# Down-projection of a decoder layer: inputs and weights get buffers of their own, splits are issued ahead, and the preparation of weight sums is spread over 16 steps per half

## The chip, the cores and the metric

One Trainium2 chip, one of its cores. The number is the device time of one execution of the whole program in microseconds (us); before, the median of 3 runs was 3280.65 us (3274.83 to 3296.78).

The engines as the profile names them: PE does the matmuls (PEld loads the 128x128 operand of one), DVE and POOL do elementwise work, ACT copies and applies functions, SP issues the DMAs. Each executes its own instructions in program order and waits on semaphores of the others.

## The reference

A decoder layer on x of 2048 x 1024 in float32: four token mixers, an output projection, a layer norm, and then the feed-forward part, which is what the change touches:

```python
ALPHA = (2.0 * DEPTH) ** 0.25
x = _layer_norm(ALPHA * x + mix, ln1_w[l], ln1_b[l])
h = jnp.square(jax.nn.relu(x @ w_up[l]))            # w_up: 1024 x 4096
x = _layer_norm(ALPHA * x + h @ w_down[l], ln2_w[l], ln2_b[l])   # w_down: 4096 x 1024
```

## The kernel before

**Stages.** The mixers, the output projection and the first norm take the span up to about 1815 us. The up-projection follows in two halves of the tokens (`ffn_up(0)` and `ffn_up(1)`, 16 steps each), then the down-projection (`ffn_down`, 32 steps), which begins with its first matmul at 2518.87 us and whose last matmul ends near 3279.4 us.

**Strassen-Winograd.** Both projections use one level of it: 7 block products P1 to P7 instead of 8. The combinations of h that the products need are written to DRAM by the up-projection as `H7[half][product]` (the profile calls these arrays H0P and H1P). Four of the seven weight operands are sums of blocks of w_down: `ffn_t(f)` loads four raw tiles for one row block f, adds on DVE and POOL, and stores four tiles into `TD` (TDP in the profile). It is called 16 times between steps of the up-projection, 4 times in the first half (s = 12 to 15) and 12 times in the second (s = 1 to 12).

**Float32 by two parts.** A 128x512 float32 tile is split: a copy on ACT makes the high part (`hh`, `z`, `x0h`, `x1h`; line 135), and a subtraction on DVE, every third time on POOL, makes the low part (`hl`, `z`, `x0l`, `x1l`; line 115). A product is then 4 blocks of the contraction x 3 matmuls (hi·hi, hi·lo, lo·hi) = 12 matmuls of 128x512 into one PSUM bank.

**A step of `ffn_down`.** Step i has half i//16, v = i%16//4 (which quarter of the contraction) and p = i%4 (which pair of token tiles). It runs the products in the order P1, P6, P2, P7, P5, P4, P3; product number m = 7i + 0..6. Each product needs one input tile of H7 (raw tile by DMA, then split) and four weight tiles (8 with their low parts), which stay for 4 steps; the products change their weights at different steps (`OFF`). The weights' split tiles are not double-buffered: 16 pairs x1 for P1, P6, P4, P3 and 12 pairs x0 for P2, P7, P5. Over 32 steps there are 7 + 16 + 16 + 16 = 55 changes of 4 tiles. P1's result is copied to SBUF on ACT (`wh<-bank`), the others go through 7 DVE operations that read a bank, and 4 adds on POOL, into the y tiles. At v = 0 the y tiles are loaded with x; at v = 3 `lnorm2` normalises and stores both token tiles (ACT squares, 8 DVE operations, a power on POOL).

**What sets the order.** Tiles come from pools by name and rotate through a fixed number of places; an instruction that writes a place waits until the place's earlier readers are done. In `ffn_down` all raw tiles, inputs and weights alike, rotate through 7 places (3 named `xr`, 4 named `wl`; line 1389 issues the DMA). `prod` issues the load and the split of its own input directly ahead of its matmuls; behind the matmuls of the last product that uses a set of weights it issues loads and splits of the next set. Input splits go by turns to two `z2` tiles and to 6 pairs `hh`/`hl`. A scheduler may move instructions when the program is built.

Of the kernel before, what the change touches and what calls it, by code (L numbers as in the profile page):

```python
# [18 lines left out]
P = 128  # L19
# [65 lines left out]
class Body:  # L85
# [1205 lines left out]
        W["P3"] = put(a12)  # L1291
        return W

    def ffn_up(self, hf, X, between):

        fw = self.fw
        XN = {"P1": "B11", "P2": "B21", "P3": "B22", "P4": "T4", "P5": "T1", "P6": "T2", "P7": "T3"}

        def prod(W, n):
            ps = self.slot("pu", [P, 512])  # L1300
            wh, wl = W[n]
            for k in range(4):
                xh, xl = X[XN[n]][k]
                ks = slice(k * P, k * P + P)
                for i, (a, b) in enumerate(((wh, xh), (wh, xl), (wl, xh))):
                    self.mm(ps, a[:, ks], b, start=(k == 0 and i == 0), stop=(k == 3 and i == 2))
            return ps

        def relu2(r):
            self.act(r, r, AF.Relu)  # L1310
            self.act(r, r, AF.Square)

        for s in range(16):
            def out(n, r):
                self.nc.sync.dma_start(self.H7[hf][n][s // 4][:, :, s % 4, :], r.rearrange("p (q t) -> p q t", q=4))

            W = self.ffn_w(s)
            c11, u2, u3, c22 = (self.t(fw, n, [P, 512], bufs=i) for n, i in (("q1", 2), ("u2", 2), ("u3", 1), ("c", 1)))
            self.copy("a", c11, prod(W, "P1"))
            self.add("v", u2, c11, prod(W, "P6"))  # L1320
            self.add("v", c11, c11, prod(W, "P2"))
            relu2(c11)
            out("P1", c11)
            p5 = prod(W, "P5")
            self.add("v", u3, u2, prod(W, "P7"))
            self.add("v", u2, u2, p5)
            self.add("v", c22, u3, p5)
            relu2(c22)
            out("P4", c22)
            self.add("v", u3, u3, prod(W, "P4"))  # L1330
            relu2(u3)
            out("P2", u3)
            self.add("v", u2, u2, prod(W, "P3"))
            relu2(u2)

            self.add("v", c22, u2, c22)
            out("P5", c22)
            self.sub("g", u2, c11, u2)
            out("P7", u2)
            self.sub("v", c11, c22, c11)  # L1340
            out("P6", c11)
            self.sub("g", u3, u3, c11)
            out("P3", u3)
            between(s)

    def ffn_t(self, f):

        nc, w = self.nc, self.ap["w_down"]
        b12, t1, b22 = self.raw(w[f][:, 512:]), self.raw(w[f][:, :512]), self.raw(w[f + 16][:, 512:])
        b21 = self.t(self.of, "x1t", [P, 2, 512], bufs=1)[:, 0]  # L1350
        nc.sync.dma_start(b21, w[f + 16][:, :512])
        self.sub("v", t1, b12, t1)
        nc.sync.dma_start(self.TD["P5"][f], t1)
        self.sub("g", b12, b22, b12)
        nc.sync.dma_start(self.TD["P7"][f], b12)
        self.sub("v", b22, b22, t1)
        nc.sync.dma_start(self.TD["P6"][f], b22)
        self.sub("g", b21, b21, b22)
        nc.sync.dma_start(self.TD["P4"][f], b21)

# [3 lines left out]
    def ffn_down(self):  # L1366
# [5 lines left out]
        with ExitStack() as es:  # L1372
            fs = es.enter_context(tc.tile_pool(name="fs", bufs=1, side="right"))
            stat = self.t(fs, "st2", [P, 504])[:, :32].rearrange("p (t j) -> p t j", j=2)
            fd = es.enter_context(tc.tile_pool(name="fd", bufs=1, side="right", reuse_waits="tile"))
            ys = [self.t(fd, f"y2_{n}", [P, 512]) for n in range(5)]
            nraw, nh = [0], [0]

            def hpair():
                nh[0] += 1  # L1380
                if nh[0] % 8 < 2:
                    z = self.t(of, "z2", [P, 2, 512], F32R, bufs=2)
                    return z[:, 0], z[:, 1]
                return [self.t(fd, x, [P, 512], F32R, bufs=6) for x in ("hh", "hl")]

            def raw(src):
                nraw[0] += 1
                r = self.t(*((self.fr, "xr") if nraw[0] % 7 < 3 else (of, "wl")), [P, 512], bufs=3 if nraw[0] % 7 < 3 else 4)
                nc.sync.dma_start(r, src)
                return r  # L1390

            W = {}

            def load_w(n, c):
                W[n] = []
                for f in range(4 * c, 4 * c + 4):
                    if n in self.TD:
                        src = self.TD[n][f]
                    else:
                        src = self.ap["w_down"][f + 16 * (n != "P1")][:, 512 * (n == "P3") : 512 * (n == "P3") + 512]  # L1400
                    W[n].append(self.split_to(wtag(n), raw(src)))

            def prod(n, i):
                ps = self.slot("py", [P, 512])
                hi, lo = hpair()
                self.split(raw(self.H7[i // 16][n][chunk(n, i)][:, i % 4].rearrange("p s t -> p (s t)")), hi, lo)
                for k in range(4):
                    ks = slice(k * P, k * P + P)
                    wh, wl = W[n][k]
                    for m, (x, w) in enumerate(((hi, wh), (hi, wl), (lo, wh))):  # L1410
                        self.mm(ps, x[:, ks], w, start=(k == 0 and m == 0), stop=(k == 3 and m == 2))
                if i + 1 < nsteps and chunk(n, i + 1) != chunk(n, i):
                    load_w(n, chunk(n, i + 1))
                return ps

            for n in ("P1", "P6", "P2", "P7", "P5", "P4", "P3"):
                load_w(n, chunk(n, 0))
                if n == "P6":
                    lns = self.t(of, "ln1", [P, 2, D], bufs=1)
                    nc.sync.dma_start(lns, self.ap["lns"][2:4].partition_broadcast(P))  # L1420
            self.t(fd, "hh", [P, 512], F32R, bufs=6)
            self.t(fd, "hl", [P, 512], F32R, bufs=6)
            ys += [self.t(fd, f"y2_{n}", [P, 512]) for n in range(5, 14)]
            two = self.t(of, "x1t", [P, 2, 512], bufs=1)
            ys += [two[:, 0], two[:, 1]]
            for i in range(nsteps):
                hf, v, p = i // 16, i % 16 // 4, i % 4
                y = [[ys[4 * p + 2 * l + j] for j in range(2)] for l in range(2)]
                tl = [8 * hf + 4 * l + p for l in range(2)]
                if v == 0:  # L1430
                    for l in range(2):
                        for j in range(2):
                            nc.sync.dma_start(y[l][j], self.x1[tl[l]][:, 512 * j : 512 * j + 512])

                def acc(l, j, ps, first=True, last=True):
                    self.stt(y[l][j], y[l][j], ALPHA if first and v == 0 else 1.0, ps, ALU.mult, ALU.add,
                             stat[:, tl[l], j : j + 1] if last and v == 3 else None)

                def both(l, j, ps, u):
                    if v == 0:  # L1440
                        acc(l, j, ps)
                    self.add("g", y[l][j], y[l][j], u)
                    if v:
                        acc(l, j, ps)

                t, u2, u3 = (self.t(of, "wh", [P, 512], bufs=4) for _ in range(3))
                self.copy("a", t, prod("P1", i))
                self.add("v", u2, t, prod("P6", i))
                both(0, 0, prod("P2", i), t)
                self.add("v", u3, u2, prod("P7", i))  # L1450
                p5 = prod("P5", i)
                acc(0, 1, p5, last=False)
                self.add("g", y[0][1], y[0][1], u2)
                both(1, 1, p5, u3)
                both(1, 0, prod("P4", i), u3)
                acc(0, 1, prod("P3", i), first=False)
                if v == 3:
                    for l in range(2):
                        self.lnorm2(tl[l], y[l], stat[:, tl[l], :], lns)
# [20 lines left out]
def body(ctx, tc, ap, seq=SEQ):  # L1480
# [34 lines left out]
    def run(it):  # L1515
        for _ in it:
            pass
# [47 lines left out]
    with ExitStack() as e1:  # L1565
        B.t(pool("pad", e1, side="right"), "pad", [P, 504])
        B.fw = pool("fw", e1, side="right", reuse_waits="tile")
        X1 = B.ffn_x1()
        B.ffn_up(0, X, lambda s: run(B.out_final(11 + s)) if 0 < s < 5 else next(X1) if 7 < s < 12 else B.ffn_t(s) if s > 11 else None)
        B.ffn_up(1, next(X1), lambda s: B.ffn_t(s - 1) if 0 < s < 13 else None)  # L1570
    B.ffn_down()
    ef.close()

# [79 lines left out]
```

## Time and profile before

| | |
|---|---|
| median of 3 runs | 3280.65 us (3274.83 to 3296.78) |
| profiled execution | 3298.5 us, its span 3296.7 us |
| mean granted TensorE clock | 0.916 |
| PE busy | 2966.6 us (90%), 15524 matmuls |
| DVE / POOL / ACT busy | 2161.5 / 1550.9 / 1333.2 us |
| DMA | 513.69 MB, mean 156 GB/s |
| up-projection, second half | about 2186 to 2502.5 us |
| down-projection, first to last matmul | 2518.87 to 3279.4 us |

The profile's rows give, for a group of equal instructions, how often it ran, its busy time, the mean duration of one, and how long the engine stood idle just before them and on whom it waited. In a view by windows each engine has its busy time (with the count of instructions) in a stretch of the span, then the granted clock, the DMA share and GB/s. Busy PE time is not PE at its full rate: after a wait matmuls are recorded with longer durations, and the spacing of their starts tells the rate.

### The profile page before, as it was taken

The numbers are of one execution on the slowest core, as the hardware profiler recorded it, in microseconds if no ns is written. First come the engines' busy times: TensorE is split into PE (matmuls) and PEld (weight loads), VectorE is DVE, ScalarE is ACT, GpSimd is POOL, SyncE is SP. The second block draws the span as 40 slices with busy tenths as digits, with TensorE's granted clock in tenths as the row PEclk, the third lists the DMA queues.
The fourth block names the chain that finished last, engine by engine and source line by source line (L and its number), as shares of the span: only waits on it lengthen the run. The fifth ranks groups of instructions, "written<-read, shape, count | busy, mean of one in ns | idle before, by whom it ended". The sixth has DMA issues, their size and how long they took to land. (4 is left out here: it accounts for less than half of the span.)

```text
span 3296.7 us, 46483 instructions
## 1 busy us (share of the span) xinstructions
PE 2966.6 (90%) x15524; PEld 2381.6 (72%) x15524; DVE 2161.5 (66%) x3828; ACT 1333.2 (40%) x2878; POOL 1550.9 (47%) x1432
## 2 busy tenths in 40 slices
PE   8899988998999998999996998989997889888887
PEld 6667776777787787877775786767785667676665
DVE  3567589688677856334457667777766655776568
ACT  3344334433433442343344444453455333443333
POOL 1333366366355455002226446566554555556455
PEclk9899798998799998899997999999998999999998
DMA  5343323423334354434555568678758545665544
GB/s 168 121 129 100 93 91 104 130 92 102 87 99 114 108 174 151 129 124 132 168 179 165 158 200 248 192 243 283 234 160 274 160 148 163 193 204 160 160 157 137
DMA packets 406656, 513.69 MB, mean 156 GB/s; under 512 B 34321, under 2 KB 234129, under 8 KB 406161
## 3 DMA queue, kind: packets, MB, share of 16 engines
q1 hardware_dynamic: 406416, 510.72, 49.9%
q8 instruction: 123, 2.02, 0.3%
q14 instruction: 117, 0.95, 0.1%
HBM read 354.69 MB, written 155.91 MB: 155 GB/s over the span
## 5 line engine op out<-in xcount | busy, mean ns | idle before, releaser
L112 PE MATMUL mm<-xh,wh 128*128 128x512 f32 x672 | 283.1, 423 | 30.4 <-ACT xh L135 15.8
L112 PE MATMUL mm<-xl,wh 128*128 128x512 f32 x672 | 283.6, 422 | 7.5 <-DVE xl L115 4.6
L112 PE MATMUL mm<-xh,wl 128*128 128x512 f32 x672 | 280.9, 418 | 3.3 <-DVE wl L115 3.1
L115 POOL TENSOR_TENSOR y<-y,wh 128x512 f32<-128x512 f32 x112 | 165.3, 1486 | 115.8 <-DVE y L128 38.9
L135 ACT ACTIVATE wh<-raw 128x512 fp32r<-128x512 f32 (+1 forms) x220 | 136.7, 629 | 173.1 <-PE mm L112 74.8
L112 PE MATMUL bank<-x0h,wh 128*128 128x512 f32 x384 | 159.1, 415 | 40.7 <-DVE c L115 35.8
L112 PEld LDWEIGHTS mm<-xh,wh 128*128 128x128 f32 x672 | 133.5, 199 | 69.9 <-ACT xh L135 19.2
L112 PE MATMUL bank<-x1h,hh 128*128 128x512 f32 x384 | 154.8, 403 | 20.9 <-ACT hh L135 20.9
L115 DVE TENSOR_TENSOR wl<-raw,wh 128x512 fp32r<-128x512 f32 (+1 forms) x146 | 121.4, 836 | 73.6 <-ACT wh L135 70.9
L115 POOL TENSOR_TENSOR wl<-raw,wh 128x512 fp32r<-128x512 f32 (+1 forms) x74 | 103.7, 1402 | 132.5 <-ACT wh L135 114.1
L112 PEld LDWEIGHTS mm<-xl,wh 128*128 128x128 f32 x672 | 134.1, 200 | 42.0 <-DVE xl L115 7.4
L112 PE MATMUL mm<-wh,xh 128*128 128x256 f32 (+1 forms) x512 | 158.2, 312 | 3.1 <-ACT stg L131 2.0
L112 PE MATMUL mm<-wl,xh 128*128 128x256 f32 (+1 forms) x512 | 157.2, 308 | 3.5 <-DVE wl L115 3.3
L112 PEld LDWEIGHTS mm<-xh,wl 128*128 128x128 f32 x672 | 133.8, 199 | 35.7 <-DVE wl L115 4.7
L112 PE MATMUL bank<-x1h,hl 128*128 128x512 f32 x384 | 152.8, 401 | 6.9 <-DVE hl L115 4.8
L112 PE MATMUL bank<-x0h,hh 128*128 128x512 f32 x288 | 122.3, 424 | 39.0 <-ACT hh L135 38.9
L112 PE MATMUL bank<-x0l,wh 128*128 128x512 f32 x384 | 156.4, 408 | 0.0
L112 PE MATMUL bank<-x0h,wl 128*128 128x512 f32 x384 | 156.1, 406 | 0.0
L112 PE MATMUL mm<-wh,xl 128*128 128x256 f32 (+1 forms) x512 | 154.5, 303 | 0.0
L112 PE MATMUL bank<-x1l,hh 128*128 128x512 f32 x384 | 153.8, 401 | 0.0
L112 PE MATMUL bank<-x1l,wh 128*128 128x512 f32 x384 | 150.7, 393 | 2.2 <-DVE x1l L115 2.1
L112 PE MATMUL bank<-x1h,wh 128*128 128x512 f32 x384 | 150.3, 391 | 2.2 <-ACT q L135 2.2
(471 smaller groups left out, 8941.5 us busy)
## 6 DMA issues: line engine op xcount, KB each, us to landing
raw<-in_w_ch SPq DMA_DIRECT2D x140, 256.0 KB, 3.0
wr<-in_w_up SPq DMA_DIRECT2D x128, 256.0 KB, 3.2
xr<-in_w_down SPq DMA_DIRECT2D x100, 256.0 KB, 4.2
xr<-TDP SPq DMA_DIRECT2D x78, 256.0 KB, 3.3
wl<-H0P SPq DMA_DIRECT2D x76, 256.0 KB, 3.7
wl<-H1P SPq DMA_DIRECT2D x75, 256.0 KB, 3.6
chF<-stg SPq DMA_DIRECT2D x68, 256.0 KB, 2.4
xraw<-in_xT SPq DMA_DIRECT2D x64, 256.0 KB, 3.6
```

The lines of the kernel that those rows point to most:

```text
L112: return self.nc.tensor.matmul(out, lhsT, rhs, start=start, stop=stop)
L115: (self.nc.gpsimd if eng == "g" else self.nc.vector).tensor_tensor(out, a, b, op=op)
L135: self.nc.scalar.activation(out, in_, AF.Copy)
```

## The change

In `ffn_down`:

- The raw inputs get 7 places of their own (3 `xr`, and 2 `z2` tiles of two halves), the raw weights the 4 `wl` places. Split inputs always go to the 6 `hh`/`hl` pairs.
- `prod(m)` issues the split of input m+4 and the load of input m+10 ahead of its own matmuls.
- A list `change` fixes for each new set of weights at which product it is loaded (`a`) and split (`b`): split two products behind its last use at the earliest, and at least three products behind the split of the set before it.
- The first seven sets are loaded in another order, partly into other places, and four input splits stand between them.
- The y tiles are multiplied by ALPHA on ACT right behind their load (8 steps with 4 copies each), so that the first sum no longer carries the factor; the POOL add and the DVE sum of one y tile now always come in the same order.

In the up-projection, `ffn_t` becomes a generator whose 16 row blocks are each cut in two pieces (four loads; sums and stores). It is advanced at the end of a step (`between`) and, newly, in the step's middle (`mid`, behind the output of P1): 6 row blocks in the first half and 10 in the second.

```diff
-    def ffn_t(self, f):
+    def ffn_t(self):
...
+        for f in (12, 13, 14, 15, *range(12)):
+            b12, t1, b22 = self.raw(w[f][:, 512:]), self.raw(w[f][:, :512]), self.raw(w[f + 16][:, 512:])
+            b21 = self.t(self.of, "x1t", [P, 2, 512], bufs=1)[:, 0]
+            nc.sync.dma_start(b21, w[f + 16][:, :512])
+            yield
+            self.sub("v", t1, b12, t1)
...
+            nc.sync.dma_start(self.TD["P4"][f], b21)
+            yield
...
-            nraw, nh = [0], [0]
-            def hpair():
...
-            def raw(src):
-                nraw[0] += 1
-                r = self.t(*((self.fr, "xr") if nraw[0] % 7 < 3 else (of, "wl")), [P, 512], bufs=3 if nraw[0] % 7 < 3 else 4)
...
+            def load_h(m):
+                i, n = seq[m]
+                if m % 7 < 3:
+                    r = self.t(self.fr, "xr", [P, 512], bufs=3)
+                else:
+                    if m % 7 in (3, 5):
+                        raws["z"] = self.t(of, "z2", [P, 2, 512], bufs=2)
+                    r = raws["z"][:, (m % 7 - 3) % 2]
+                nc.sync.dma_start(r, self.H7[i // 16][n][chunk(n, i)][:, i % 4].rearrange("p s t -> p (s t)"))
+                raws[m] = r
+            def split_h(m):
+                if m < len(seq):
+                    H[m] = [self.t(fd, x, [P, 512], F32R, bufs=6) for x in ("hh", "hl")]
+                    self.split(raws.pop(m), *H[m])
...
+            change, at = [], -3
+            for m, (i, n) in enumerate(seq):
+                if i + 1 < nsteps and chunk(n, i + 1) != chunk(n, i):
+                    prev, at = at, max(m + 2, at + 3)
+                    change.append((max(prev + 1, m - 6, 0), at, n, chunk(n, i + 1)))
+            def prod(m):
+                i, n = seq[m]
+                split_h(m + 4)
+                load_h(m + 10)
+                for a, b, w, c in change:
+                    if a == m:
+                        raws[w] = list(load_w(w, c))
+                    if b == m:
+                        split_w(w, raws.pop(w))
                 ps = self.slot("py", [P, 512])
-                hi, lo = hpair()
-                self.split(raw(self.H7[i // 16][n][chunk(n, i)][:, i % 4].rearrange("p s t -> p (s t)")), hi, lo)
+                hi, lo = H.pop(m)
...
-                if i + 1 < nsteps and chunk(n, i + 1) != chunk(n, i):
-                    load_w(n, chunk(n, i + 1))
...
-            for n in ("P1", "P6", "P2", "P7", "P5", "P4", "P3"):
-                load_w(n, chunk(n, 0))
+            places = ("xr", "xr", "wl", "wh", "wl", "wh", "wl")
+            for n, place in zip(("P1", "P6", "P2", "P5", "P7", "P4", "P3"), places):
...
+                            self.act(y[l][j], y[l][j], AF.Copy, scale=ALPHA)
...
-                    self.stt(y[l][j], y[l][j], ALPHA if first and v == 0 else 1.0, ps, ALU.mult, ALU.add,
+                    self.stt(y[l][j], y[l][j], 1.0, ps, ALU.mult, ALU.add, stat[:, tl[l], j : j + 1] if last and v == 3 else None)
...
-        B.ffn_up(1, next(X1), lambda s: B.ffn_t(s - 1) if 0 < s < 13 else None)
+        loads = (2, 3, 4, 5, 7, 8, 9, 11, 12, 13)
+        B.ffn_up(1, next(X1), lambda s: next(T) if s in loads else None, lambda s: next(T) if s - 1 in loads else None)
```

Three places in the instruction order show what moves. The first is ACT around step 8 of `ffn_down`, before: `wh_23781<-bank_63` copies the result of product 56 (P1); `hh_23826` is the high part of the input of product 57, `hh_23869` that of product 58, and `x1h` are high parts of weights.

```order
L135 ACTIVATE hh_23826<-wl_23828 128x512
L135 ACTIVATE x1h_23803<-xr_23801 128x512
L135 ACTIVATE x1h_23809<-wl_23807 128x512
L135 ACTIVATE x1h_23815<-wl_23813 128x512
L135 ACTIVATE x1h_23821<-wl_23819 128x512
L135 ACTIVATE wh_23781<-bank_63 128x512
L135 ACTIVATE x1h_23846<-xr_23844 128x512
L135 ACTIVATE x1h_23852<-xr_23850 128x512
L135 ACTIVATE x1h_23858<-xr_23856 128x512
L135 ACTIVATE hh_23869<-wl_23871 128x512
```

After, at the same place, `wh_23835<-bank_63` is the copy of product 56, and the input splits that stand ahead of it are those of products 61 (`hh_23857`) and 62 (`hh_23876`).

```order
L135 ACTIVATE hh_23857<-z_4266_23693 128x512
L135 ACTIVATE x1h_23882<-wl_23814 128x512
L135 ACTIVATE x1h_23886<-wl_23816 128x512
L135 ACTIVATE x1h_23890<-wl_23818 128x512
L135 ACTIVATE hh_23876<-z_4266_23693 128x512
L135 ACTIVATE wh_23835<-bank_63 128x512
L135 ACTIVATE x1h_23894<-wl_23820 128x512
L135 ACTIVATE x1h_23966<-wl_23917 128x512
```

So before one input split stood ahead of that copy, and six stand ahead of it now, counted in products behind number 56.

The second is the queue of SP with the loads for the same products, before; the last row but two of this piece (`wl_23871`) is the input of product 58, and it stands behind loads of weights (in_w_down, TDP) that share its places.

```order
L1389 DMA xr_23785<-H0P_1_15374 128x512
L1389 DMA xr_23801<-in_w_down 128x512
L1389 DMA xr_23844<-TDP_8_15469 128x512
L1389 DMA wl_23819<-in_w_down 128x512
L1389 DMA xr_23850<-TDP_9_15470 128x512
L1389 DMA wl_23828<-H0P_1_15394 128x512
L1389 DMA wl_23862<-TDP_11_15472 128x512
L1389 DMA xr_23856<-TDP_10_15471 128x512
L1389 DMA wl_23871<-H0P_1_15378 128x512
L1389 DMA wl_23891<-H0P_2_15399 128x512
L1389 DMA wl_23910<-H0P_1_15390 128x512
```

After, the first three rows are the inputs of products 56, 57 and 58, in `xr`; the weights behind them go to `wl` only.

```order
L1395 DMA xr_23568<-H0P_1_15374 128x512
L1395 DMA xr_23590<-H0P_1_15394 128x512
L1395 DMA xr_23609<-H0P_1_15378 128x512
L1411 DMA wl_23649<-in_w_down 128x512
L1411 DMA wl_23651<-in_w_down 128x512
L1411 DMA wl_23653<-in_w_down 128x512
L1411 DMA wl_23655<-in_w_down 128x512
L1395 DMA z_4257_23647<-H0P_2_15399 128x512
L1395 DMA z_4257_23647<-H0P_1_15390 128x512
L1411 DMA wl_23730<-TDP_8_15485 128x512
```

An input's load now waits for earlier inputs alone, and a weight's load for earlier weights, though both still stand in one queue.

The third is DVE right behind the up-projection's last sum with a bank, after: low parts of weights (`x0l`, `x1l`), the last two sums of h (`c`, `q`), and the low part of the first input (`hl_22220`).

```order
L115 TENSOR_TENSOR x0l_22260<-wl_22251,x0h_22259 128x512
L115 TENSOR_TENSOR x0l_22264<-wl_22253,x0h_22263 128x512
L115 TENSOR_TENSOR x0l_22272<-wl_22257,x0h_22271 128x512
L115 TENSOR_TENSOR x1l_22292<-wh_22283,x1h_22291 128x512
L115 TENSOR_TENSOR x1l_22296<-wh_22285,x1h_22295 128x512
L115 TENSOR_TENSOR c_22007<-u_3834_22005,c_22007 128x512
L115 TENSOR_TENSOR x1l_22304<-wh_22289,x1h_22303 128x512
L115 TENSOR_TENSOR q_3833_22004<-c_22007,q_3833_22004 128x512
L115 TENSOR_TENSOR x1l_22316<-wl_22307,x1h_22315 128x512
L115 TENSOR_TENSOR x1l_22324<-wl_22311,x1h_22323 128x512
L115 TENSOR_TENSOR x1l_22328<-wl_22313,x1h_22327 128x512
L115 TENSOR_TENSOR hl_22220<-xr_22205,hh_22219 128x512
```

So eleven DVE operations now stand between that last sum and the first input's low part.

More of the change, by code (lines that the diff above doesn't have):

```diff
@@ L1292, in ffn_w, with ffn_up @@
         return W
-    def ffn_up(self, hf, X, between):
+    def ffn_up(self, hf, X, between, mid):
         fw = self.fw
@@ L1323, in ffn_up @@
             out("P1", c11)
+            mid(s)
             p5 = prod(W, "P5")
@@ L1344, in ffn_up @@
             between(s)
-    def ffn_t(self, f):
+    def ffn_t(self):
         nc, w = self.nc, self.ap["w_down"]
[L1349 to L1359, printed above, removed]
+        for f in (12, 13, 14, 15, *range(12)):
[4 more added lines that the diff above has]
+            self.sub("v", t1, b12, t1)
+            nc.sync.dma_start(self.TD["P5"][f], t1)
+            self.sub("g", b12, b22, b12)
+            nc.sync.dma_start(self.TD["P7"][f], b12)
+            self.sub("v", b22, b22, t1)
+            nc.sync.dma_start(self.TD["P6"][f], b22)
+            self.sub("g", b21, b21, b22)
+            nc.sync.dma_start(self.TD["P4"][f], b21)
+            yield
     OFF = {"P1": 1, "P6": 1, "P2": 2, "P4": 2, "P5": 3, "P3": 3, "P7": 0}
@@ L1376, in ffn_down, with load_w @@
             ys = [self.t(fd, f"y2_{n}", [P, 512]) for n in range(5)]
-            nraw, nh = [0], [0]
-            def hpair():
[L1380 to L1384, printed above, removed]
-            def raw(src):
-                nraw[0] += 1
-                r = self.t(*((self.fr, "xr") if nraw[0] % 7 < 3 else (of, "wl")), [P, 512], bufs=3 if nraw[0] % 7 < 3 else 4)
[L1389 to L1395, printed above, removed]
+            raws, W, H = {}, {}, {}
+            seq = [(i, n) for i in range(nsteps) for n in ("P1", "P6", "P2", "P7", "P5", "P4", "P3")]
+            def load_h(m):
+                if m >= len(seq):
+                    return
+                i, n = seq[m]
[11 more added lines that the diff above has]
+                    self.split(raws.pop(m), *H[m])
+            def load_w(n, c, place=None):
                 for f in range(4 * c, 4 * c + 4):
@@ L1400, in load_w, with split_w @@
                         src = self.ap["w_down"][f + 16 * (n != "P1")][:, 512 * (n == "P3") : 512 * (n == "P3") + 512]
-                    W[n].append(self.split_to(wtag(n), raw(src)))
-            def prod(n, i):
+                    r = self.raw(src) if place == "xr" else self.t(of, place or "wl", [P, 512], bufs=4)
+                    if place != "xr":
+                        nc.sync.dma_start(r, src)
+                    yield r
+            def split_w(n, rs):
+                W[n] = [self.split_to(wtag(n), r) for r in rs]
+            change, at = [], -3
[12 more added lines that the diff above has]
+                        split_w(w, raws.pop(w))
                 ps = self.slot("py", [P, 512])
-                hi, lo = hpair()
-                self.split(raw(self.H7[i // 16][n][chunk(n, i)][:, i % 4].rearrange("p s t -> p (s t)")), hi, lo)
+                hi, lo = H.pop(m)
                 for k in range(4):
@@ L1409, in prod @@
                     wh, wl = W[n][k]
-                    for m, (x, w) in enumerate(((hi, wh), (hi, wl), (lo, wh))):
-                        self.mm(ps, x[:, ks], w, start=(k == 0 and m == 0), stop=(k == 3 and m == 2))
-                if i + 1 < nsteps and chunk(n, i + 1) != chunk(n, i):
-                    load_w(n, chunk(n, i + 1))
-                return ps
-            for n in ("P1", "P6", "P2", "P7", "P5", "P4", "P3"):
-                load_w(n, chunk(n, 0))
-                if n == "P6":
+                    for q, (x, w) in enumerate(((hi, wh), (hi, wl), (lo, wh))):
+                        self.mm(ps, x[:, ks], w, start=(k == 0 and q == 0), stop=(k == 3 and q == 2))
+                return ps
+            places = ("xr", "xr", "wl", "wh", "wl", "wh", "wl")
+            for n, place in zip(("P1", "P6", "P2", "P5", "P7", "P4", "P3"), places):
+                if place == "xr":
+                    W[n] = [self.split_to(wtag(n), r) for r in load_w(n, chunk(n, 0), place)]
+                else:
+                    split_w(n, list(load_w(n, chunk(n, 0), place)))
+                if n == "P2":
+                    for m in range(7):
+                        load_h(m)
                     lns = self.t(of, "ln1", [P, 2, D], bufs=1)
                     nc.sync.dma_start(lns, self.ap["lns"][2:4].partition_broadcast(P))
-            self.t(fd, "hh", [P, 512], F32R, bufs=6)
-            self.t(fd, "hl", [P, 512], F32R, bufs=6)
+                    split_h(0)
+                    split_h(1)
+                elif n == "P7":
+                    split_h(2)
+                    split_h(3)
+            for m in (7, 8, 9):
+                load_h(m)
             ys += [self.t(fd, f"y2_{n}", [P, 512]) for n in range(5, 14)]
@@ L1433, in ffn_down, with acc @@
                             nc.sync.dma_start(y[l][j], self.x1[tl[l]][:, 512 * j : 512 * j + 512])
-                def acc(l, j, ps, first=True, last=True):
-                    self.stt(y[l][j], y[l][j], ALPHA if first and v == 0 else 1.0, ps, ALU.mult, ALU.add,
[L1437 to L1444, printed above, removed]
-                t, u2, u3 = (self.t(of, "wh", [P, 512], bufs=4) for _ in range(3))
[L1447 to L1452, printed above, removed]
-                self.add("g", y[0][1], y[0][1], u2)
-                both(1, 1, p5, u3)
-                both(1, 0, prod("P4", i), u3)
-                acc(0, 1, prod("P3", i), first=False)
+                            self.act(y[l][j], y[l][j], AF.Copy, scale=ALPHA)
+                def acc(l, j, ps, last=True):
+                    self.stt(y[l][j], y[l][j], 1.0, ps, ALU.mult, ALU.add, stat[:, tl[l], j : j + 1] if last and v == 3 else None)
+                t, u2, u3 = (self.t(of, "wh", [P, 512], bufs=4) for _ in range(3))
+                m = 7 * i
+                self.copy("a", t, prod(m))
+                self.add("v", u2, t, prod(m + 1))
+                self.add("g", y[0][0], y[0][0], t)
+                acc(0, 0, prod(m + 2))
+                self.add("g", y[0][1], y[0][1], u2)
+                self.add("v", u3, u2, prod(m + 3))
+                p5 = prod(m + 4)
+                self.add("g", y[1][1], y[1][1], u3)
+                acc(0, 1, p5, False)
+                acc(1, 1, p5)
+                self.add("g", y[1][0], y[1][0], u3)
+                acc(1, 0, prod(m + 5))
+                acc(0, 1, prod(m + 6))
                 if v == 3:
@@ L1568, in body @@
         X1 = B.ffn_x1()
-        B.ffn_up(0, X, lambda s: run(B.out_final(11 + s)) if 0 < s < 5 else next(X1) if 7 < s < 12 else B.ffn_t(s) if s > 11 else None)
-        B.ffn_up(1, next(X1), lambda s: B.ffn_t(s - 1) if 0 < s < 13 else None)
+        T = B.ffn_t()
+        B.ffn_up(0, X, lambda s: run(B.out_final(11 + s)) if 0 < s < 5 else next(X1) if 7 < s < 12 else None if s == 15 else next(T) if s > 4 else None,
+                 lambda s: next(T) if s in (6, 7, 8) or s > 12 else None)
+        loads = (2, 3, 4, 5, 7, 8, 9, 11, 12, 13)
+        B.ffn_up(1, next(X1), lambda s: next(T) if s in loads else None, lambda s: next(T) if s - 1 in loads else None)
     B.ffn_down()
```

## The prediction

> **What bounds the kernel now.** I began with the page's head and its slices, to see whether the stage that the change touches (2518.9 to 3279.4 us, the last nine slices) looks like the rest.
>
> ```profile
> span 3296.7 us, 46483 instructions
> PE 2966.6 (90%) x15524; PEld 2381.6 (72%) x15524; DVE 2161.5 (66%) x3828; ACT 1333.2 (40%) x2878; POOL 1550.9 (47%) x1432
> ...
> PE   8899988998999998999996998989997889888887
> ...
> PEclk9899798998799998899997999999998999999998
> ```
>
> PE is busy in every slice, so the mean tells nothing: what counts is how near to its rate PE runs. For that I cut the two projections into stretches. Per stretch the view gives length, then busy time and count of PE, PEld, DVE, ACT and POOL, then the granted clock, the DMA share and GB/s.
>
> ```profile
> core 0: us, PE busy (x) PEld busy (x) DVE busy (x) ACT busy (x) POOL busy (x), PEclk, DMA share, GB/s
> 2186.00:2345.00 159.00, 140.49 (x573) 112.25 (x572) 119.43 (x131) 60.18 (x108) 100.27 (x68) 0.94 0.87 281
> 2354.00:2490.00 136.00, 135.74 (x593) 111.43 (x594) 94.24 (x117) 70.93 (x123) 68.16 (x48) 1.00 0.54 159
> 2502.50:2518.90 16.40, 0.23 (x2) 0.03 (x1) 14.92 (x17) 12.94 (x23) 10.95 (x8) 0.61 0.93 294
> 2518.90:3279.40 760.50, 669.03 (x2678) 524.22 (x2679) 491.75 (x643) 296.12 (x531) 409.45 (x288) 0.93 0.54 173
> 2714.20:2807.60 93.40, 82.90 (x337) 65.46 (x336) 53.55 (x66) 34.66 (x61) 48.84 (x35) 0.93 0.51 159
> 2807.60:2909.00 101.40, 88.08 (x342) 67.80 (x341) 81.05 (x128) 45.19 (x90) 57.22 (x42) 0.92 0.65 211
> ```
>
> The second row is the yardstick: a late piece of the up-projection in which PE never stands still, at a granted clock of 1.00: 136.00 us for 593 matmuls of the same 128x512 shape, **0.2293 us each**. The down-projection runs 32 steps x 7 products x 12 = 2688 matmuls (2678 are recorded). At the yardstick they would take 616.4 us; the stage takes 760.5. So **144.1 us** of it are lost, at DMA 0.54, DVE 65%, POOL 54%, ACT 39%: no engine and no queue is full. This is a stage of waits, and the waits of PE in that stretch say for whom:
>
> ```profile
> PE bank L112 <- ACT hh L135: 59.8, 21, 6.2
> PE bank L112 <- ACT z L135: 30.0, 8, 16.2
> PE bank L112 <- DVE z L115: 6.3, 5, 2.3
> PE bank L112 <- DVE hl L115: 6.2, 4, 2.4
> PE bank L112 <- POOL hl L115: 3.1, 4, 1.4
> PE bank L112 <- POOL z L115: 1.4, 1, 1.4
> ```
>
> All six name one thing, an input split that came late; no row names weights. The 16.2 us wait is that of the first matmul and lies ahead of the stage, so 106.8 - 16.2 = 90.6 us of the loss are plain waiting. The other 53.5 us must be rate. What a stall does to the rate is seen at product 58 in step 8:
>
> ```profile
> 2719.35 0.63 ACT L135 ACTIVATE hh<-wl 128x512 fp32r<-128x512 f32 x1 [1.65 <-DMA wl<-H0P]
> 2720.03 0.80 PE L112 MATMUL bank<-x0h,hh 128*128 128x512 f32 x1 [4.51 <-ACT hh L135]
> 2720.62 0.63 PE L112 MATMUL bank<-x0l,hh 128*128 128x512 f32 x1
> 2721.07 0.80 PE L112 MATMUL bank<-x0h,hh 128*128 128x512 f32 x1
> 2721.67 0.63 PE L112 MATMUL bank<-x0l,hh 128*128 128x512 f32 x1
> ```
>
> After the stall, matmuls start 0.45 to 0.60 us apart, twice the yardstick and more, and the granted clock of the stage is 0.93 against 1.00. [...]
>
> And why is the split late? ACT's own waits in the stage:
>
> ```profile
> ACT hh L135 <- DMA wl<-H0P: 97.0, 38, 6.5
> ACT hh L135 <- DMA wl<-H1P: 94.6, 34, 6.3
> ACT hh L135 <- DMA xr<-H1P: 47.5, 21, 5.6
> ACT hh L135 <- DMA xr<-H0P: 44.1, 18, 5.6
> ```
>
> ACT stands 283 us before input loads. These loads are not slow by themselves:
>
> ```profile
> wl<-H0P SPq DMA_DIRECT2D x76, 256.0 KB, 3.7
> ```
>
> 3.7 us from issue to landing is little more than one product (12 x 0.2293 = 2.75 us). They are issued late: the place of the raw tile is freed only by splits of weights, which wait for the last use of the old weights. The order rows show it: the load of product 58 stands behind loads of weights into the same seven places, and only one input split stands ahead of P1's copy.
>
> **The change, part by part.** *Splits ahead, places apart.* Nothing is taken off PE, and the counts of splits and loads stay the same. The splits of inputs stand six products ahead on ACT at P1's copy in every step (16.5 us), instead of one at each fourth step. Cover against a late load of 3.7 us is thus plentiful, and both the 90.6 us and the 53.5 us should go; what is late next must be priced.
>
> *What is late next: the steps with the norm.* In the 8 steps with v = 3 (the last row of the windows is one group of four) DVE has 81.05/4 = 20.3 us of work per step, against 84 x 0.2293 = 19.3 us for PE. DVE becomes the bound there, and it also waits for ACT's squares and POOL's power inside the norm. At 90% busy a step takes 22.5 us, 3.3 over PE's, 26 us for eight; each group of four enters with some lead, for which I take off one product, 6 us for two groups: **20 us**. Bounds: 0 (the lead covers it all) and 8 x (25.35 - 19.3) = 48 us (they stay as they are). In the other 24 steps DVE has 53.55/4 = 13.4 and POOL 48.84/4 = 12.2 us, well under 19.3.
>
> *Weights.* There are 55 changes of 4 tiles, each split at the earliest two products after its last use, with at most one set in the raw places at a time. Loads of the next set can start when the former's low parts are done. Four loads of 3.7 us that overlap take some 6 us, two products, and three products lie between two changes, so a set comes at most a product late, behind five products of splits already done. I keep **8 us**, about half of the 17.0 us that the four rows of DVE and POOL show now (bounds 0 and 17).
>
> *The factor ALPHA on ACT.* 32 more copies, priced by the splits of the same tile:
>
> ```profile
> L135 ACT ACTIVATE hh<-wl 128x512 fp32r<-128x512 f32 x110 | 68.8, 630 | 194.3 <-DMA wl<-H0P 97.0 <-DMA wl<-H1P 94.6 <-DVE wh L115 2.3
> y<-x SPq DMA_DIRECT2D x28, 256.0 KB, 4.5
> ```
>
> 32 x 0.63 = 20.2 us on an engine that would be busy 316 of 644 us. They add a wait: ACT stands until y has landed, 4.5 us and for four tiles rather 6, and behind it in line are later input splits and P1's copy. The six products of lead hide it, so nothing; without that cover 8 steps x 4.5 = 36 us. The new order of POOL's adds and DVE's sums changes no count: 0, within plus or minus 3.
>
> Down: 616.4 + 20 + 8 = 644.4 us, **116.1 less**.
>
> *The start of the stage.* PE now stands 16.4 us between the projections:
>
> ```profile
> 2502.31 0.39 PE L112 MATMUL bank<-x1h,wl 128*128 128x512 f32 x1
> ...
> 2518.87 0.79 PE L112 MATMUL bank<-x1h,z 128*128 128x512 f32 x1 [16.17 <-ACT z L135]
> ```
>
> After, the inputs are loaded long before, but eleven DVE operations still stand between the last sum and the first low part. By this window's own mean (14.92/17 = 0.88 us) twelve take 10.5 us, so about 11: **5 less**, bounds 13 less (ACT's high parts alone) and 0.
>
> *The sums of weights.* The SP and DVE work of `ffn_t` is the same 16 blocks; two move from the second half to the first. In 2186 to 2354 us, where it runs now, PE loses time to a chain through DVE:
>
> ```profile
> PE bank L112 <- DVE c L115: 16.6, 6, 6.2
> ```
>
> Halved pieces may spread this, or bring it into the first half, where there was room for only four blocks. I take **0**, plus or minus 10.
>
> The sum is 121 us off the profiled execution: 3298.5 - 121 = 3177.5 us. That execution is 17.9 us above the median, 0.5%, without a stage that I could name; scaled by 3280.65/3298.5 it gives **3160 us**.
>
> **The rivals.** *B: DVE and POOL hinder one another more when the steps are shorter.* The low parts already take longer than the sums that read a bank:
>
> ```profile
> L128 DVE SCALAR_TENSOR_TENSOR y<-y,bank 128x512 f32<-128x512 f32 x142 | 94.6, 679 | 21.3 <-PE bank L112 16.3 <-POOL y L115 4.8
> L115 DVE TENSOR_TENSOR x1l<-wl,x1h 128x512 fp32r<-128x512 f32 x37 | 46.6, 1275 | 3.7 <-ACT x1h L135 3.7
> L115 POOL TENSOR_TENSOR hl<-wl,hh 128x512 fp32r<-128x512 f32 x35 | 49.5, 1414 | 47.1 <-ACT hh L135 46.5 <-DMA wl<-H1P 0.4
> ```
>
> 0.68 us with one operand in a bank, 1.28 with two in SBUF. If such DVE operations never run beside POOL's, a plain step has 13.4 - 7 x 0.68 = 8.6 us of them and 12.2 us of POOL, one after the other 20.8 us, more than PE's 19.3; with norm steps as now that is 24 x 20.8 + 8 x 25.35 = 702 us, 58.5 less, with the start 63.5 less: **3217 us**. Against it: busy time may hold the waiting already, and then the pair counts it twice. [...]
>
> *C: it doesn't do what it says.* SP is one queue still; a weight load that waits for its place holds every input load behind it. If inputs stay late, the 59.8 + 30.0 - 16.2 = 73.6 us behind ACT remain with their part of the lost rate, 53.5 x 73.6/90.6 = 43.5 us, and 27 of the 144 us are gained: **3254 us**. Against it: ten products lie between load and use.
>
> *D, slower: four places for raw weights are too few.* Where a set is split late, PE stands at the product that uses it, once per change. To end 1% above now, PE must lose 144 + 5 + 33 = 182 us in 55 changes, 3.3 us each: from there on it is **slower, 3314 us**. It decides if four weight loads together take over three products plus the lead of five, 22 us; a 3.7 us landing speaks against that.
>
> **How the numbers follow.** Forecast 0.66, B 0.22, C 0.08, D 0.04. The low end is the floor: all 144 us gone, 13 at the start, 10 in the up-projection, 3114 us. The high end takes in B with 10 us lost in the up-projection, 3227 us. A measurement tells about 1% from no change, 33 us: faster holds the forecast and B, 0.88; C falls within, 0.08; slower 0.04.
>
> **What would show it.** Right: the stage takes 635 to 660 us, PE's waits for `hh` on ACT nearly vanish, plain steps take 19.3 to 20 us at a clock near 1.00, norm steps 21 to 24, and PE's first wait is 8 to 13 us. For B: plain steps of 20.5 us or more, with PE waiting for `hl` on DVE or POOL and those rows longer than 0.92 and 1.41. For C: ACT still waits for H0P and H1P by the hundred. For D: PE waits that name `x0h`, `x1l`. I would be wrong if the up-projection lost over 20 us to the new places of `ffn_t`.

## The result, and the profile after

The changed kernel takes **3164.11 us** (median of 4 runs, 3151.5 to 3174.24) against 3281.2 us of before (also 4 runs now); the ratio is 0.9635, 95% interval 0.9585 to 0.9684. In a later comparison, again beside the kernel before, it took 3157.89 us, ratio 0.9629 (0.9586 to 0.9672). The forecast was 3160 us.

The page's head and slices of the kernel after, to set beside those of before:

```profile
span 3159.0 us, 46740 instructions
PE 2910.0 (92%) x15524; PEld 2362.1 (75%) x15524; DVE 2193.9 (69%) x3828; ACT 1353.0 (43%) x2910; POOL 1571.1 (50%) x1432
...
PE   8889989889899999899998699898999899999997
...
PEclk9899798987999999699998799999999899999998
```

PE's busy time fell by 57 us with the same count of matmuls: that part is rate, not waiting. The last slices, 8 and 9 mixed before, are now nearly all 9. By windows, first the up-projection before; then, after, the up-projection, the whole down-projection, its start, 8 plain steps of it, and steps 13 to 15 with the norm:

```profile
1777.10:2502.50 725.40, 670.39 (x2818) 540.56 (x2818) 521.34 (x636) 324.76 (x579) 405.30 (x309) 0.96 0.69 212
```

```profile
1770.90:2493.40 722.50, 667.39 (x2818) 540.13 (x2818) 532.03 (x639) 328.00 (x585) 404.44 (x310) 0.95 0.69 215
2505.90:3137.40 631.50, 618.32 (x2688) 507.68 (x2688) 507.59 (x635) 314.14 (x561) 432.84 (x288) 0.99 0.64 206
2505.90:2534.10 28.20, 25.48 (x99) 20.37 (x100) 21.17 (x23) 19.46 (x36) 19.23 (x13) 0.84 0.98 342
2591.30:2743.60 152.30, 152.30 (x674) 126.15 (x673) 112.23 (x131) 71.38 (x121) 106.30 (x70) 1.00 0.62 194
2763.10:2838.40 75.30, 69.36 (x297) 56.13 (x296) 70.49 (x102) 41.55 (x85) 47.39 (x33) 0.98 0.71 228
```

The up-projection is unchanged (725.4 and 722.5 us). The down-projection takes 631.5 us; its granted clock rose from 0.93 to 0.99. In the plain steps PE never stops: 8 steps are 672 matmuls (the view's 674 counts two that were still running when the window begins), 152.30/672 = 0.2266 us each, and every start follows the one before by 226 or 227 ns. At the start, 99 matmuls take 28.2 us, 5.8 more than at that rate, at a granted clock of 0.84. In the norm's steps DVE is busy 70.49 of 75.30 us. PE's waits in the stage:

```profile
PE bank L112 <- ACT hh L135: 12.3, 1, 12.3
PE bank L112 <- DVE hl L115: 4.5, 3, 2.7
PE bank L112 <- DVE st L1503: 3.3, 2, 2.3
PE bank L112 <- DVE wh L115: 2.1, 2, 1.3
PE bank L112 <- DVE st L1504: 1.8, 1, 1.8
PE bank L112 <- DVE y L128: 1.3, 1, 1.3
```

The 12.3 us are the one wait ahead of the first matmul (16.17 before). Inside the stage 13 us are left of 90.6. ACT now waits for other things:

```profile
ACT hh L135 <- PE bank L112: 144.9, 82, 2.1
ACT y L131 <- DMA y<-x: 43.6, 14, 7.2
ACT x1h L135 <- DMA wl<-in_w_down: 33.4, 20, 11.7
ACT x1h L135 <- DMA wl<-TDP: 31.1, 25, 4.9
```

No input load is among them: ACT waits for PE to give back a split pair, that is, it is as far ahead as the six pairs allow.

The last matmul starts at 3281.65 us before and 3137.19 after:

```profile
3281.65 0.40 PE L112 MATMUL bank<-x1h,z 128*128 128x512 f32 x1
```

```profile
3137.19 0.39 PE L112 MATMUL bank<-x1h,hl 128*128 128x512 f32 x1
```

So 15.0 us of the span stand behind it before, and 21.8 after. Of the profiled difference of 137.7 us, the down-projection (first to last start, 762.8 to 631.2) gives 131.5, the wait ahead of it 3.8, the up-projection 2.8, the stages ahead of that 6.3, and the tail takes 6.8 back.

### The profile page after: what moved, and what is told of

Its sections match the earlier page's. It is cut to its first block, busy times and chain, and to the rows that moved or that the text cites. A ratio compares the mean times of both kernels' runs of the same rounds, so it can differ in the third digit from the quotient of the medians.

```text
span 3159.0 us, 46740 instructions
## 1 busy us (share of the span) xinstructions
PE 2910.0 (92%) x15524; PEld 2362.1 (75%) x15524; DVE 2193.9 (69%) x3828; ACT 1353.0 (43%) x2910; POOL 1571.1 (50%) x1432
## 5 line engine op out<-in xcount | busy, mean ns | idle before, releaser
L112 PE MATMUL bank<-x1h,hh 128*128 128x512 f32 x512 | 201.4, 393 | 16.9 <-ACT hh L135 12.3
L115 POOL TENSOR_TENSOR y<-y,wh 128x512 f32<-128x512 f32 x112 | 175.0, 1573 | 63.5 <-DVE wh L115 36.3
L112 PE MATMUL bank<-x1h,hl 128*128 128x512 f32 x512 | 200.9, 392 | 4.5 <-DVE hl L115 2.7
L112 PE MATMUL bank<-x1l,hh 128*128 128x512 f32 x512 | 200.9, 392 | 0.0
L112 PE MATMUL bank<-x0h,hh 128*128 128x512 f32 x384 | 150.4, 392 | 2.2 <-DVE y L128 1.3
L112 PE MATMUL bank<-x0h,hl 128*128 128x512 f32 x384 | 150.3, 392 | 1.8 <-DVE hl L115 1.8
```

The lines of the kernel that those rows point to most:

```text
L112: return self.nc.tensor.matmul(out, lhsT, rhs, start=start, stop=stop)
L115: (self.nc.gpsimd if eng == "g" else self.nc.vector).tensor_tensor(out, a, b, op=op)
```

## The experiments

**Three parts of the down-projection put back** (places, set-ahead, late renewal of weights):

```diff
-                split_h(m + 4)
-                load_h(m + 10)
+                split_h(m)            # its load, too, into one of 7 shared places
...
-                    prev, at = at, max(m + 2, at + 3)
-                    change.append((max(prev + 1, m - 6, 0), at, n, chunk(n, i + 1)))
+                    change.append((m + 1, m + 1, n, chunk(n, i + 1)))
```

> The changed kernel with three parts of the down-projection put back: inputs and weights share seven raw places again, each product issues load and split of its own input, and a set of weights is loaded and split right behind its last use. The sums of weights in 16 steps, ALPHA on ACT and the first loads stay as changed. Theory P (the loss before was input splits that came late, and these three parts removed it): about 3265 to 3285 us, the down-projection at 745 to 765 us with PE waiting for hh on ACT again. Rival R (the gain came from the other parts): under 3200 us.

Measured: 3224.53 us, ratio to before 0.9839 (0.9805 to 0.9874), the down-projection 695.9 us. Neither: about half of the gain was gone, and 53 us of it were still there. PE's waits and the stage's row:

```profile
PE bank L112 <- ACT hh L135: 67.0, 20, 10.6
2514.10:3210.00 695.90, 635.17 (x2688) 514.65 (x2688) 502.99 (x647) 315.39 (x561) 421.52 (x291) 0.95 0.60 190
```

The wait is the old one, only smaller. So what I had put back was not all that made the waits. The next two runs put back less.

**Shared places, but splits four products ahead in the program:**

```diff
-                split_h(m)
+                split_h(m + 4)
```

> As the run before (shared places, weights renewed at once), but load and split of an input stand four products ahead in the program; ACT's order then has six input splits ahead of P1's copy in every step, as in the changed kernel. Theory O (it is the order on ACT and SP that counts): 3160 to 3180 us, down-projection 630 to 650 us. Theory Q (own places are needed, since an input's load still waits for weights that hold the places): over 3200 us, down-projection over 665 us, with ACT waiting for input loads by the hundred us.

Measured: 3153.54 us, ratio 0.9616 (0.9582 to 0.965), down-projection 629.1 us: theory O, even a little under its range. **Own places are not needed.** (This run also keeps the changed kernel's four input splits between the first weights; the run before did not.) The ACT waits for H1P loads in this run sum to 35.8 us in the two largest rows, and PE hardly sees them: of its 20.4 us for `hh`, 16.7 are the wait ahead of the first matmul.

```profile
PE bank L112 <- ACT hh L135: 20.4, 4, 16.7
ACT hh L135 <- PE bank L112: 149.5, 87, 2.1
ACT y L131 <- DMA y<-x: 29.0, 11, 5.9
ACT hh L135 <- DMA wl<-H1P: 23.9, 14, 4.3
ACT hh L135 <- DMA xr<-H1P: 11.9, 8, 3.1
```

**Own places, but no split set ahead in the program and weights renewed at once** (inputs are still loaded six products ahead):

```diff
-                split_h(m + 4)
-                load_h(m + 10)
+                split_h(m + 0)
+                load_h(m + 6)
...
+                    change.append((m + 1, m + 1, n, chunk(n, i + 1)))
```

> The changed kernel with its own places for inputs and weights, but each product issues the split of its own input and a set of weights is loaded and split right behind its last use. ACT's order has again six input splits ahead of P1's copy. Theory O and theory Q: both 3160 to 3180 us. Rival S (the renewal of weights two products later and three apart is what keeps ACT from standing): over 3200 us.

Measured: 3159.86 us, ratio 0.9639 (0.9612 to 0.9666), down-projection 634.3 us. Setting the splits ahead in the program is not needed either, once the places are apart; own places with inputs loaded no earlier than they are split were not run. In both kernels the scheduler arrives at the same order on ACT, six input splits ahead of P1's copy in every step (with shared places five in the first); either edit alone lets it.

**What was left: one position.** In the run that put three parts back, a product's input was loaded ahead of the next weights (2 to 6 splits ahead of P1's copy); in the kernel before it came behind them (1 to 6). I put that back too:

```diff
-                    if b == m:
-                        split_w(w, load_w(w, c))          # behind split_h(m), ahead of the matmuls
+                if late:                                  # the set with b == m + 1, behind the matmuls of product m
+                    split_w(late[0], load_w(*late))
```

> The run that put three parts back, with one thing more put back: a new set of weights is loaded and split ahead of the next product's input instead of behind it. One to five input splits then stand ahead of P1's copy on ACT (2 to 6 before this edit), as in the kernel before. Theory I (in shared places this one position decides, each set of weights holding up one input more): 3262 to 3285 us, down-projection 745 to 765 us. Rival R2 (the 53 us that were left to the other parts come from ALPHA on ACT, the pairs, the first loads and the sums of weights): 3215 to 3235 us, no change.

Measured: 3276.83 us, ratio 1.0014 (0.9989 to 1.0039), down-projection 766.8 us. That is the kernel before again, with 52 us decided by which of two neighbours stands first:

```profile
PE bank L112 <- ACT hh L135: 93.0, 29, 7.9
2490.00:3256.80 766.80, 671.01 (x2688) 529.03 (x2688) 491.56 (x645) 310.22 (x561) 409.46 (x292) 0.92 0.54 172
```

On ACT, mostly 1, 5, 5 and 4 input splits stand ahead of P1's copy in four steps, against 2, 6, 6 and 4 in the run with three parts back.

This run also prices everything that the kernel still has from the change (ALPHA on ACT, six pairs only, the order of sums, the first loads, the sums of weights in 16 steps): together nothing, within 0.4%. That holds for a kernel whose inputs come late; where they come early, only the sums of weights were taken back alone, below.

**The same position alone, in the kernel before:**

```diff
-                    load_w(n, chunk(n, i + 1))
+                    pend.append((n, chunk(n, i + 1)))     # loaded and split behind the next input's split
```

> The kernel before with one edit: a new set of weights is loaded and split behind the load and split of the next product's input instead of ahead of them. Theory I: 3215 to 3240 us, down-projection 690 to 715 us. Rival R2: 3270 to 3285 us.

Measured: 3229.93 us, ratio 0.9855 (0.9826 to 0.9884), down-projection 718.2 us. The time is as theory I said, the stage 3 us above its range: this one position gives 40% of the change's gain (45 of 117 us). The scheduler moved other splits with it, so that 1 to 8 stand ahead of P1's copy in the built order.

**The sums of weights back at their old places:**

```diff
-        B.ffn_up(1, next(X1), lambda s: next(T) if s in loads else None, lambda s: next(T) if s - 1 in loads else None)
+        B.ffn_up(1, next(X1), lambda s: (next(T), next(T)) if 0 < s < 13 else None, lambda s: None)
```

> The changed kernel with the sums of weights at their old places (4 row blocks in the first half of the up-projection, 12 in the second, each in one piece). If their spreading is worth nothing, as the prediction had it: 3150 to 3175 us, the up-projection within 8 us of 722 us. If it carries a part of the gain: over 3180 us.

Measured: 3159.22 us, ratio 0.9633 (0.9612 to 0.9655), up-projection 723.7 us. The spreading is worth nothing that shows.

**The lead itself cut:**

```diff
-                    H[m] = [self.t(fd, x, [P, 512], F32R, bufs=6) for x in ("hh", "hl")]
+                    H[m] = [self.t(fd, x, [P, 512], F32R, bufs=2) for x in ("hh", "hl")]
```

> The changed kernel with 2 pairs hh/hl instead of 6, so that at most two input splits stand ahead of P1's copy, while loads stay early and places stay apart. If the lead in splits is what hides the waits of ACT (for y, for raw weights, for the last use of old weights): 3200 to 3260 us, the down-projection 665 to 725 us, PE waiting for hh on ACT. If early loads alone do it: 3155 to 3180 us.

Measured: 3214.69 us, ratio 0.9807 (0.9782 to 0.9832), down-projection 698.4 us. The lead is what hides the waits, but PE waits mostly for another half than I wrote:

```profile
PE bank L112 <- DVE hl L115: 31.0, 27, 3.7
PE bank L112 <- ACT hh L135: 20.5, 10, 11.3
PE bank L112 <- POOL hl L115: 9.4, 10, 3.6
```

11.3 us of the second row are the start. With two pairs the low parts on DVE and POOL are late; the loads are early.

**The norm's multiply-adds left out:**

```diff
-            self.stt(y, y, stat[:, 0:1], lns[:, 0, cs], ALU.add, ALU.mult)
-            self.stt(y, y, stat[:, 1:2], lns[:, 1, cs], ALU.mult, ALU.add)
```

> The changed kernel without the eight multiply-adds of the norm in each step with v = 3 (the output is left without scale and shift). If the eight norm steps are bound by DVE: the down-projection falls from 631 to 608 to 617 us and the tail behind the last matmul from 22 to 8 to 14 us, together 20 to 35 us less, 3130 to 3145 us. If PE loses its time there to something else (POOL, the clock): less than 8 us less.

Measured: 3123.56 us, ratio 0.9524 (0.9497 to 0.955). The stage falls to 617.8 us, DVE from 507.6 to 449.0, and the last matmul starts 6.6 us ahead of the span's end:

```profile
2496.90:3114.70 617.80, 613.25 (x2688) 505.83 (x2688) 449.02 (x595) 315.61 (x561) 428.51 (x292) 0.99 0.67 213
```

```profile
3114.47 0.39 PE L112 MATMUL bank<-x1h,hl 128*128 128x512 f32 x1
...
span 3121.1 us, 46702 instructions
```

So the norm's multiply-adds cost 13.7 us of PE's time and some 15 us of tail, 29 together, within the range for a bound by DVE. The total fell below its range: in this profile the up-projection also began 12.7 us earlier than in that of the changed kernel, which the edit does not explain. The 13.7 us do not spread over the eight steps. From one P1's first matmul to the next, the changed kernel takes 19.0 us in each of the steps 1 to 14, then 23.1, 24.9 and 24.5 in steps 15 to 17; of the second four only the last is longer (19.8), and what DVE is behind by then becomes tail.

**Two ways to relieve DVE there**, beside the changed kernel again:

> The changed kernel again, as the reference for the next two: 3150 to 3170 us.

Measured: 3157.89 us, ratio 0.9629 (0.9586 to 0.9672).

```diff
-        self.sub("g" if self.rr % 3 == 0 else "v", lo, raw, hi.bitcast(F32))
+        self.sub("g" if self.rr % self.gp == 0 else "v", lo, raw, hi.bitcast(F32))   # gp = 2 around and in v = 3
```

> The changed kernel, with every second instead of every third low part on POOL around and in the steps with v = 3. If DVE's amount of work bounds these steps and POOL has room (17 of 25 us busy): 5 to 15 us less than the changed kernel, norm steps 22 to 24 us instead of 25. If DVE and POOL hinder one another there as in rival B: within 4 us or slower, with DVE rows for low parts over 1.2 us.

Measured: 3161.02 us, ratio 0.9627 (0.9595 to 0.966): no gain. The norm's multiply-adds on DVE, in the kernel before, in the changed kernel beside this run, and in this run:

```profile
L128 DVE SCALAR_TENSOR_TENSOR y<-y,st,ln 128x512 f32<-128x512 f32 x56 | 52.6, 961 | 5.7 <-ACT ya L131 3.7 <-POOL st L115 1.5
```

```profile
L128 DVE SCALAR_TENSOR_TENSOR y<-y,st,ln 128x512 f32<-128x512 f32 x56 | 58.9, 1081 | 9.2 <-ACT ya L131 5.1 <-POOL st L115 3.9
```

```profile
L128 DVE SCALAR_TENSOR_TENSOR y<-y,st,ln 128x512 f32<-128x512 f32 x56 | 69.2, 1258 | 7.6 <-ACT ya L131 6.5 <-POOL st L115 0.9
```

The rows that I had named (low parts over 1.2 us) hardly grew, by 4% at most, and stayed under 1.2. These grew by 16%, behind 12% that the change itself had brought; with the norm's other eight, on `x1t` (9.3 us, then 6.8), it is 7.8 us in all. POOL took over 23 low parts, an estimated 25 us of DVE's time at the 1.01 to 1.16 us that their rows give; DVE's busy time fell by 9.6 us (2182.7 to 2173.1), and the down-projection took 637.0 us against 632.3 beside it.

Why they grew is in the trace. Their mean mixes two kinds, as DVE's rows and POOL's at the same time show, from the changed kernel beside this run:

```profile
2782.98 0.74 DVE L128 SCALAR_TENSOR_TENSOR y<-y,st,ln 128x512 f32<-128x512 f32 x1
2784.83 4.13 DVE L128 SCALAR_TENSOR_TENSOR y<-y,st,ln 128x512 f32<-128x512 f32 x3 [0.45 <-POOL st L115]
```

```profile
2784.76 1.29 POOL L115 TENSOR_TENSOR y<-y,wh 128x512 f32<-128x512 f32 x1
2786.03 1.72 POOL L115 TENSOR_TENSOR hl<-xr,hh 128x512 fp32r<-128x512 f32 x1
```

The three of the second row take 1.77, 1.77 and 0.74 us. The first two begin while a 128x512 operation of POOL runs, and they end 0.55 us behind its end; the third begins when POOL is done. So it is throughout: 15 of the 64 multiply-adds begin beside such an operation in the kernel before, 23 in the changed kernel beside this run, 32 in this run, and each of these ends 0.545 to 0.556 us behind POOL's, while no other takes longer than 0.76 us. Most low parts do the same (in the first profile of the changed kernel 0.67 to 0.70 us alone, and of the 183 that begin beside such an operation 167 end 0.53 to 0.57 us behind it), while DVE operations with one operand in a bank stay at 0.67 to 0.69 us beside POOL. So in these runs a multiply-add that meets an operation of POOL waits until that one has ended, and with more low parts on POOL there were more of these waits (32 against 23).

```diff
+            if j:
+                self.act(y, y, AF.Copy, scale=stat[:, 1:2])
+                self.add("g", y, y, lns[:, 1, cs])
+            else:
                 self.stt(y, y, stat[:, 1:2], lns[:, 1, cs], ALU.mult, ALU.add)
```

> The changed kernel, with the last multiply-add of the norm for the second half of each row done as a scaling on ACT and an add on POOL. DVE loses 2 of 8 multiply-adds per norm step, 2.2 us. If DVE's amount of work bounds these steps: 8 to 18 us less than the changed kernel, part of it in the tail. If the chain within the norm or POOL binds: within 5 us.

Measured: 3152.2 us, ratio 0.9604 (0.9572 to 0.9636). It is 5.7 us under the changed kernel's median, and the intervals overlap: not shown to be faster. The stage takes 630.2 us and the tail 22.4, against 632.3 and 21.8 beside it, so the tail did not shrink as expected; of the 48 multiply-adds left on DVE, 25 begin beside an operation of POOL and wait for its end. No run here is clearly faster than the changed kernel among those that compute the reference.

## Why the prediction was right, point by point

- **The floor.** Right in kind, 7 us too high: the yardstick of 0.2293 us came from a stretch of the up-projection in which a third of the matmuls start 230 to 236 ns apart and most others 226 or 227; plain steps now run at 0.2266, 609 us for 2688 matmuls.
- **The size of the loss.** I ended the stage at 3279.4 us and took ten matmuls for unrecorded. They lie behind that: the last starts at 3281.65, and the stage was 762.8 us by starts.
- **Both parts of the loss go.** Right: 90.6 us of waits became 13, and the other 53.5 us, the rate, went with them. That it would was my estimate from the row of product 58; what lowers the rate behind a wait, no run shows. Runs with a part of the waits have a part of the rate: clock 0.92 with 93.0 us of waits for `hh`, 0.95 with 67.0, 0.99 with the start's alone. The granted clock is not the whole of it: with two pairs, 53 us of waits inside the stage, those for low parts 3.7 us at the longest, leave the clock at 0.98, and still 36 us are lost beyond waits and floor. The same sum gives 63 us for the kernel before, where I had 53.5, because the floor is lower than I took it.
- **Why.** Half right. That input splits came late because they stood behind weights, and that a lead of six cures it, is shown (two pairs cost about 55 us). But I credited own places and set-ahead together; **either one suffices** (own places with loads six products ahead, or splits four ahead in shared places), since what counts is the order on ACT and SP that comes out, and 45 to 52 us hang on a single position, the next input ahead of the new weights instead of behind. ACT's order and SP's were not changed one without the other, except that two pairs lose 55 us though the loads are early.
- **The norm steps.** The term was 20 us. It measured 13.7 in the stage; but DVE's backlog also ends the program: the tail grew by 6.8 us, for which my sum had no term. Together 20.5: the total was met by two sizes, not one. The steps themselves did not shorten to 22.5 us: between starts of P1's copy, which follow the pace of ACT and DVE, the norm steps take 24.6 to 26.0 us, while PE first uses up its lead and stands later, in steps 15 to 17.
- **Weights.** 8 us allowed, nothing found: no wait of PE names `x0h` or `x1l`, and renewal at once is as good. The 17.0 us from which I took it were no measure of weights: all four rows name low parts of inputs.
- **ALPHA.** ACT waits 43.6 us for y and the lead hides all of it, as said; with the other leftovers it sums to nothing. It was not run alone.
- **The start.** 5 us forecast, 3.8 measured (12.7 between matmul starts against 16.6).
- **The sums of weights.** 0 forecast, and 0 within the comparison's uncertainty.
- **The profile's 17.9 us over the median.** I could not place them. The first matmul of the up-projection starts at 1777.1 us in the profile of before and between 1755.8 and 1779.3 in those of the other kernels, which do the same work up to there: much of it may lie ahead of the feed-forward part. The profiled difference, 137.7, is 20.6 us larger than that of the medians, 117.1. In this pair of profiles 9.1 us of it lie ahead of the down-projection (6.3 and 2.8), outside the change; the rest I cannot place.
- **The rivals.** B as priced (3217 us) did not come: plain steps are PE's alone. But its mechanism exists, and it is shown for the norm's multiply-adds, whose mean went from 0.96 us before to 1.08 after and 1.26 with more on POOL: they take 0.73 to 0.76 us, or else wait until POOL's operation has ended and end 0.55 us behind it. The price failed for the reason that I had suspected: DVE's rows hold these waits already, so adding POOL's time counted them twice. C and D did not happen.

In the profiled executions the sum fell short, 121 us forecast and 137.7 measured. The floor (7), the weights (8), the norm inside the stage (6) and the stages ahead (9) took less time than the sum had; on the other side stand the 5.8 us of slow start inside the stage and the 6.8 us of tail, for which it had no terms. That the medians agree to 4 us is therefore partly luck: the profiled execution of before lay 17.9 us above its median, the one after 3.4 below. By the later comparison the medians differ by 124.7 us, so a gain of some 120 us holds.

## What to carry to other kernels

When an in-order engine feeds another, count in the built order how many of the next products' preparations stand ahead of each instruction that can wait; here one split fewer in most steps (1, 5, 5, 4 against 2, 6, 6, 4) was worth 50 us, and six in every step another 60. Before buffers are added for that, try to change the order alone: shared places with the inputs issued ahead were as good as places of their own. And when PE's waits go, look for the next engine at the end of the program too, where its backlog becomes tail (here 6.8 us more). Before work goes from DVE to POOL, look at DVE's rows beside POOL's in the timeline: one mean can hide operations that wait for the other engine (here 1.08 us, of which those that did not wait took 0.73 to 0.76).

## What was not expected of the hardware

Handing DVE's work to POOL in the norm steps returned nothing: the remaining multiply-adds became 16% longer (1081 to 1258 ns), because 32 of 64 instead of 23 began beside an operation of POOL and ended only 0.55 us behind it. And with no stalls the plain steps run matmuls 0.2266 us apart, 1.2% closer than the stretch of the up-projection that looked undisturbed, the yardstick; elsewhere the kernel before reaches the same 0.2267 over 200 matmuls from 2095 us on. Why a third of the yardstick's matmuls come 230 to 236 ns apart stays open.
